# A hybrid encoder block on one core: DeltaNet scalings spread over half tiles, norm sums moved, w_out's raw buffers and the last norm's order

## The chip, the cores and the metric

The kernel runs on one core of a Trainium2 chip. The metric is the device time of one execution in microseconds (us); less is better. A core has the engines TensorE (PE, matmul; PEld is its weight load), VectorE (DVE), ScalarE (ACT), GpSimd (POOL) and SyncE (SP, which issues most transfers), each with an instruction stream of its own that it works off in order; semaphores tie the streams together. The transfers themselves are done by 16 DMA engines.

## The reference

One layer on 1024 positions of width 1024, in float32, and a last RMSNorm:

```python
h = rmsnorm(x, norm_mix_w)
qa, ka, va, za, ba, aa, qb, kb, vb, ga, gb = split(h @ w_in)
qa, ka, va = split(silu(causal_dwconv(cat(qa, ka, va), conv_qkv_w)))     # 4 heads of 128
qa, ka = l2norm(qa), l2norm(ka); beta = sigmoid(ba); g = -exp(a_log) * softplus(aa + dt_bias)
oa = rmsnorm(gated_delta_rule(qa, ka, va, g, beta), gdn_norm_w) * silu(za)
ob = chunk_band_attention(qb, kb, vb, rel_bias)                          # 8 heads of 64
x = x + (sigmoid(ga) * (oa @ w_branch_a) + sigmoid(gb) * (ob @ w_branch_b)) @ w_out
h = rmsnorm(x, norm_ffn_w); u = causal_dwconv(h @ w_up, conv_ffn_w) + conv_ffn_b
x = x + (silu(gate) * up) @ w_down                                       # gate, up = split(u)
return rmsnorm(x, norm_final_w)

def gated_delta_rule(q, k, v, g, beta):          # per head, chunks of 64 positions, n = 16
    G = cumsum(g); gam = exp(G)
    a_mat = beta * (k @ k.T) * exp(G_i - G_j) [i > j]
    w_c, uv_c = solve(a_mat + I, [beta * gam * k, beta * v])             # triangular
    p_c = (q @ k.T) * exp(G_i - G_j) [i >= j]; kd_c = k * exp(G_last - G)
    for each chunk:  u = uv_c - w_c @ s;  o = (q * gam) @ s + p_c @ u;  s = gam_last * s + kd_c.T @ u
```

## The kernel before, in words

Every large matmul is done as three with operands split in a high and a low part (`whi`, `wlo` of a weight, `BH`, `BL` of h). A weight tile of 128x1024 is loaded by SP (`wraw`), cast by ACT (`whi`, line 85) and subtracted by POOL (`wlo`, line 88, four instructions). Raw, high and low tiles come from one pool, `wst`, with two buffers for each of the tags `raw`, `hi` and `lo`; a load waits until the buffer that it takes has been read.

A *half tile* is 24 matmuls of 512 columns: one weight tile against half of the positions, into one `psph`. In the DeltaNet part the loop is `for h in range(-1, GH)`; in turn h the kernel emits the chain of head h, the preparation of head h+1 and, as filling between their steps, the projections and convolutions of head h+2, the output gate z of head h+1 and some branch gates. `n` counts the half tiles of a turn and `i_s = h + 1` picks from the tuples at the top of the file at which n a piece is emitted:

- `SCALE`, a dictionary by head: `gdn_scale(c, p)` (lines 555 to 561) multiplies one of eight pairs of chunks of the head's `Kd`, `Vs` and `nKs` by factors per row, four ACT instructions. A head in `SCALE` gets one p in each half tile from n on, placed behind the last `acc` or gate instruction on ACT. For a head not in it, `gdn_prep2` emits all eight behind the exponential `decT` (line 548).
- `QN`: when `gdn_qnorm` squares q (`sqq`, line 680) and sums it on PE (`psn`); `gdn_qnorm2` copies the sums (`sn`, 694) and sends them through DRAM (`dN`, `sx`, 696 and 699) to `sx`, which line 710 reads on DVE.
- `APP`, `OUT`, `LATE`: when the solved system is applied, the head's output is transposed (`oaT`) and the second decay factor is applied. Heads are counted from 0 in the code and from the first in the words here, so that the second and third head are 1 and 2.

The preparation of a head sends its matrix `nL` to DRAM (`dL`, four DMAs, line 534) and back in another layout (`Lr`, line 536). The triangular solve runs on DVE: 31 steps of `tmp` (583) and `Zt` (585), the first of which reads Lr. Between them DVE works off the chain of the head before: U (653), O (654) and S (658) for each chunk, which PE waits for in `pss` and `psws`, and the convolution: u (440), then ACT's `acc` (444), then three `acc` on DVE (446). A scheduler sets the order of each engine from priorities and dependences, so that a small move in the code moves many rows; near the end of the program the order is pinned as written.

`load_wout(k, pool)` (line 1073) loads and splits one of eight blocks of `w_out`, the last four behind the branch products (`psout` waits for their `woh`, `wol`). In the tail, the last four tiles of 128 positions get their second half's squares early and the first half's after its last matmuls; `final` (1797) makes the mean and takes the power -0.5 on POOL (`rsf`), and `finish` (1868) scales the two halves of the output (`ot`) on ACT and DVE and stores them.

Of the kernel before, what the change touches and what calls it, by code (L numbers as in the profile page):

```python
# [8 lines left out]
F32 = mybir.dt.float32  # L9
F32R = mybir.dt.float32r  # L10
BF16 = mybir.dt.bfloat16
AF = mybir.ActivationFunctionType
ALU = mybir.AluOpType
# [4 lines left out]
P = 128  # L18
D = 1024
KT = D // P  # L20
T = 1024
NT = T // P
HN = 512
# [5 lines left out]
EPS = 1e-6  # L29
# [6 lines left out]
OUT = (0, 3, 5, 3, 8)  # L36
APP = (12, 10, 10, 2)
TANH = (0,)
SCALE = {0: 2}
LATE = (9, 8, 8, 1)  # L40
APK = (4, 4, 3, None)
QN = (7, 5, 7, 5)
PR0 = 1
SOLVE0 = {3: 5, 4: 4, 5: 5, 6: 6, 7: 6, 8: 5}
GFILL = (6, 4, 5, 5, 4)
# [7 lines left out]
def hybrid_kernel(ctx: ExitStack, tc: tile.TileContext, a):  # L53
# [6 lines left out]
    def behind(key="mm"):  # L60

        return tc.issue_after(last[key])
# [3 lines left out]
    wst = ctx.enter_context(tc.tile_pool(name="wst", bufs=2))  # L66
    sml = ctx.enter_context(tc.tile_pool(name="sml", bufs=8))
# [339 lines left out]
    def zeros(t_):  # L407

        nc.sync.dma_start(t_, a["zeros"].partition_broadcast(P).rearrange("p (n t) -> p n t", t=P))
# [96 lines left out]
    def gdn_prep2(c):  # L506
# [41 lines left out]
        last["exp"] = nc.scalar.activation(decT.rearrange("p n j -> p (n j)"), psd2, AF.Exp).ins  # L548
        if h not in SCALE:
            with behind("exp"):  # L550
# [4 lines left out]
    def gdn_scale(c, p):  # L555
        h, Kd, nKs, Vs = c["h"], c["Kd"], c["nKs"], c["Vs"]
        for e in range(2):
            r = slice(e * CH, (e + 1) * CH)
            nc.scalar.activation(Kd[r, p, e, :], nKs[r, p, :], AF.Copy, scale=eg[r, 2, p, h:h + 1])
        nc.scalar.activation(nKs[:, p, :], nKs[:, p, :], AF.Copy, scale=c["nks"][:, p:p + 1])  # L560
        nc.scalar.activation(Vs[:, p, :], Vs[:, p, :], AF.Copy, scale=c["bv"][:, p:p + 1])
# [115 lines left out]
    def gdn_qnorm(c):  # L677

        sqq = gp.tile([P, NT, P], F32, tag="zs", name="sqq")
        nc.scalar.activation(sqq, c["WQ"][:, :, 64:192], AF.Square)  # L680
        psn = psc.tile([P, 256], F32, tag="c", name="psn")

        def sums():
            for j in range(4):
                mm(psn[j * 32:(j + 1) * 32], ones2[:, 0:32], sqq[:, 2 * j:2 * j + 2, :].rearrange("p n t -> p (n t)"),
                   start=True, stop=True)

        side.append(sums)
        c["psn"] = psn
# [32 lines left out]
    def gdn_out(c):  # L722
        h, O, zs = c["h"], c["O"], c["zs"]
        oaT = stg.tile([P, T], F32, tag="gt", name="oaT")
        for q in range(2):
            ps = psc.tile([P, HN], F32, tag="c", name="psoT")
            for i in range(4):
                nc.tensor.transpose(out=ps[:, i * P:(i + 1) * P], in_=O[:, 4 * q + i, :], identity=ident)
            s = slice(q * HN, (q + 1) * HN)
            pv = ps.rearrange("p (n e t) -> p n e t", e=2, t=CH)  # L730
            zv = zs[:, s].rearrange("p (n e t) -> p n e t", e=2, t=CH)
            ov = oaT[:, s].rearrange("p (n e t) -> p n e t", e=2, t=CH)
            for e in range(2):
                nc.vector.scalar_tensor_tensor(out=ov[:, :, e, :], in0=pv[:, :, 1 - e, :], scalar=gnw[:, 0:1],
                                               in1=zv[:, :, e, :], op0=ALU.mult, op1=ALU.mult)
        nc.sync.dma_start(dO[h], oaT)
# [26 lines left out]
    for h in range(-1, GH):  # L763
# [34 lines left out]
        while True:  # L798
            if h + 1 < GH and n == QN[i_s]:
                gdn_qnorm(cs[h + 1])  # L800
# [10 lines left out]
            if n == 0 and h < 0:  # L811
                for t_ in [*ptA, *zts, *(k_[:, :, j] for k_ in Kds for j in range(2))]:
                    zeros(t_)
            if h + 1 < GH and n == QN[i_s]:
                while side:
# [19 lines left out]
            if h >= 0 and n == OUT[i_s]:  # L835
                with tc.high_priority(offset=PRI), behind():
                    gdn_out(cs[h])
            if 0 <= n - SCALE.get(h + 1, n + 1) < NT:
                with behind("act"):
                    gdn_scale(cs[h + 1], n - SCALE[h + 1])  # L840
            n += 1
# [228 lines left out]
    wop = ExitStack()  # L1070
    wo1 = wop.enter_context(tc.tile_pool(name="wo1", bufs=1, reuse_waits="tile"))

    def load_wout(k, pool):
        raw = wst.tile([P, KT, P], F32, tag="raw", name="woraw")
        nc.sync.dma_start(raw.rearrange("p k c -> p (k c)"), a["w_out"][k * P:(k + 1) * P, :])
        hi = pool.tile([P, D], F32R, name=f"woh{k}")
        lo = pool.tile([P, D], F32R, name=f"wol{k}")
        split(raw.rearrange("p k c -> p (k c)"), hi, lo, nc.vector)
        return hi, lo
# [8 lines left out]
    wout = []  # L1088
# [32 lines left out]
    XT = [[xo.tile([P, 4, HN], F32R, name=f"XT{n}{x}") for x in "hl"] for n in (1, 2, 3)]  # L1121
    wo2 = wop.enter_context(tc.tile_pool(name="wo2", bufs=1, reuse_waits="tile"))
    for k in range(4, KT):
        wout.append(load_wout(k, wo2))
    psz.close()
    psx.close()
    psF = ctx.enter_context(tc.tile_pool(name="psF", bufs=8, space=PSUM, reuse_waits="tile"))
    h0, h1 = slice(0, HN), slice(HN, T)
# [4 lines left out]
    def ps_tile(name):  # L1133
        return psF.tile([P, HN], F32, tag="mm", name=name)
# [163 lines left out]
    V, S, G, Q = Pinned(nc.vector), Pinned(nc.scalar), Pinned(nc.gpsimd), Pinned(nc.sync)  # L1298
# [477 lines left out]
    fd = ctx.enter_context(tc.tile_pool(name="fd", bufs=1, reuse_waits="tile"))  # L1776
    W12.extend(fd.tile([P, HN], F32, name=f"W12_{f}") for f in range(3, FH))
    x2 = [fd.tile([P, D], F32, name=f"x2_{t}") for t in range(NT)]
# [11 lines left out]
    for b, s in (((0, 0), 6), ((1, 1), 16), ((0, 1), 27), ((1, 0), 45)):  # L1790
        for i in range(4):
            t, c = 4 * b[0] + i, slice(b[1] * HN, (b[1] + 1) * HN)
# [1 line left out]
    loads.append((50, wn, a["norm_final_w"].partition_broadcast(P)))  # L1794
    loads.sort(key=lambda x: x[0])

    def final(t, ssqs):

        ms = sml.tile([P, 1], F32, tag="ms", name="msf")
        V.tensor_scalar(out=ms, in0=ssqs[0], scalar1=1.0 / D, scalar2=EPS, op0=ALU.mult, op1=ALU.add)  # L1800
        for i, q_ in enumerate(ssqs[1:]):
            m2 = fd.tile([P, 1], F32, tag=f"ms{i}", name="msf", bufs=4)
            V.scalar_tensor_tensor(out=m2, in0=q_, scalar=1.0 / D, in1=ms, op0=ALU.mult, op1=ALU.add)
            ms = m2
        rs = sml.tile([P, 1], F32, tag="rs", name="rsf")
        G.tensor_tensor(out=rs, in0=ms, in1=mhalf[:, 0:1], op=ALU.pow)
        return rs

    s0s, ots = [], []
    jk = fd.tile([P, D], F32, name="jk")  # L1810

    def early_steps():

        for t in range(4, NT):
            s0 = fd.tile([P, 1], F32, tag="ssq0", name="ssqf", bufs=4)
            S.activation(jk[:, h1], x2[t][:, h1], AF.Square, accum_out=s0)
            s0s.append(s0)
            ot = fd.tile([P, D], F32, tag="ot2", name="ot", bufs=4)
            G.tensor_mul(ot[:, h1], x2[t][:, h1], wn[:, h1])
            ots.append(ot)  # L1820
            yield

    def norm_steps():

        ssq, rs = {}, {}
        for i in range(6):
            if i < 4:
                ssq[i] = sml.tile([P, 1], F32, tag="ssq", name="ssqf")
                S.activation(jk, x2[i], AF.Square, accum_out=ssq[i])
            if 1 <= i < 5:  # L1830
                rs[i - 1] = final(i - 1, [ssq[i - 1]])
            if i >= 2:
                t = i - 2
                ot = fd.tile([P, D], F32, tag="ot", name="ot", bufs=2)
                V.scalar_tensor_tensor(out=ot, in0=x2[t], scalar=rs[t], in1=wn, op0=ALU.mult, op1=ALU.mult)
                Q.dma_start(a["out"][t * P:(t + 1) * P, :], ot)
            yield
# [27 lines left out]
    t = NT - 1  # L1865
    V.tensor_tensor(out=x2[t][:, h0], in0=acc[0][3], in1=x2[t][:, h0], op=ALU.add)

    def finish(i, rs):
        t, ot = 4 + i, ots[i]
        S.activation(ot[:, h1], ot[:, h1], AF.Copy, scale=rs)  # L1870
        V.scalar_tensor_tensor(out=ot[:, h0], in0=x2[t][:, h0], scalar=rs, in1=wn[:, h0], op0=ALU.mult, op1=ALU.mult)
        for e in (h1, h0):
            Q.dma_start(a["out"][t * P:(t + 1) * P, e], ot[:, e])

    ssqs = [[s0] for s0 in s0s]
    rss = {}
    for i in range(4):
        t = 4 + i
        for ci, es in enumerate((h0,) if i < 3 else (slice(0, 256), slice(256, HN))):
            ps = ps_tile("psd") if i == 3 else acc[0][i]  # L1880
            for s in range(TAIL, NS):
                tc.keep_in_program_order(down_mm(ps[:, es], s, i, i == 3 and s == TAIL, s == NS - 1, es,
                                                 skip_group_check=i < 3))
            V.tensor_tensor(out=x2[t][:, es], in0=ps[:, es], in1=x2[t][:, es], op=ALU.add)
            s1 = fd.tile([P, 1], F32, tag=f"ssq1{ci}", name="ssqf", bufs=4)
            S.activation(jk[:, es], x2[t][:, es], AF.Square, accum_out=s1)
            ssqs[i].append(s1)
            if ci == 0:
                if i > 0:
                    rss[i - 1] = final(t - 1, ssqs[i - 1])  # L1890
                if i > 1:
                    finish(i - 2, rss[i - 2])
    rss[3] = final(NT - 1, ssqs[3])
    finish(2, rss[2])
    finish(3, rss[3])


def layout(inp):
# [60 lines left out]
```

## Time and profile before

| | |
|---|---|
| median of 3 runs | 1517.43 us (1517.19 to 1518.5) |
| the profiled execution | 1519.18 us; span of its instructions 1517.4 us |
| clock granted to TensorE, mean | 0.998 of full speed |
| busy: DVE, ACT, POOL | 1081.3, 724.8, 579.4 us |
| idle of PE before instructions that wait for DVE's U (L653) | 2.5 us in 5 places |

Rows of the time order read: start in us from the span's start, length in us, engine, line, operation, output<-inputs, shape, number, and in brackets the idle time before the instruction and what ended it. Rows that begin with "SPq" are transfers at their issue; rows with "DMA" have issue and time to landing. A row of the waits reads: who waits for whom, total us, times, longest. A group's row ends with busy us, mean ns of one, and idle before it.

### The profile page before, as it was taken

The page shows a single profiled execution, that of the slowest core. Times are in us where ns is not written, and L with a number is a line of the kernel's source. Part 1 is how long each engine was busy: PE and PEld are TensorE (multiplying, and loading weights), DVE is VectorE, ACT ScalarE, POOL GpSimd, SP SyncE. Part 2 cuts the span into 40 slices and gives each one's busy share as a digit, 9 for nine tenths or more (in the row PEclk, how much of TensorE's full clock was granted, in tenths as well). Part 3 has the DMA queues.
Part 4 walks back from the last instruction along what each step waited for, and adds up shares of the span by engine and source line. Part 5 has one row for each costly group of instructions (what it writes and reads, how often), then busy time and mean ns, then how long its engine had stood idle before and what let it go on. Part 6 is the DMA issues. An engine that isn't in the chain of part 4 may idle for free.

```text
span 1517.4 us, 21270 instructions
## 1 busy us (share of the span) xinstructions
PE 1500.7 (99%) x7667; PEld 1231.9 (81%) x7667; DVE 1081.3 (71%) x2161; ACT 724.8 (48%) x1412; POOL 579.4 (38%) x529
## 2 busy tenths in 40 slices
PE   9999999999999999999999999999999999999997
PEld 6878787777888888888878878888888888888886
DVE  6875857856547887966554577777777777887886
ACT  7645546373236665744223344444444444443344
POOL 1633324222110000002211278877777775223253
PEclk9999999999999999999999999999999999999999
DMA  9322221213131111215552222333333332875523
GB/s 344 104 74 67 70 77 46 78 48 117 43 107 45 37 46 37 65 63 169 174 160 104 84 88 86 104 104 105 104 104 105 104 104 81 284 261 167 179 89 141
DMA packets 84025, 165.74 MB, mean 109 GB/s; under 512 B 20160, under 2 KB 26064, under 8 KB 83920
## 3 DMA queue, kind: packets, MB, share of 16 engines
q1 hardware_dynamic: 83376, 163.34, 32.6%
q8 instruction: 60, 0.98, 0.3%
q10 hardware_dynamic: 544, 1.05, 0.2%
q14 instruction: 45, 0.37, 0.1%
HBM read 124.24 MB, written 40.12 MB: 108 GB/s over the span
## 4 chain that ended last, share of the span: by engine, by line
PE 74%; DVE 1%; ACT 1%; DMA 1%; issue 1%; POOL 0%; SPq 0%; POOLq 0%; ACTq 0%; DVEq 0%
PE psph L58 20%; PE psd L58 9%; PE pb L58 8%; PE pa L58 5%; PE psout L58 5%; PE pc L58 5%; PE psd L1641 5%; PE pb L1282 4%; PE pa L1282 3%; PE pc L1282 3%; PE pso L58 2%; PE pss L58 2%; PE psp L996 2%; PE pst L1170 0%; PE psws L58 0%
## 5 line engine op out<-in xcount | busy, mean ns | idle before, releaser
L88 POOL TENSOR_TENSOR wlo<-wraw,whi 128x256 fp32r<-128x256 f32 x132 | 107.3, 841 | 453.9 <-ACT whi L85 452.6
L58 PE MATMUL psph<-BH,whi 128*128 128x512 f32 x656 | 263.4, 402 | 0.7 <-DVE gt L188 0.4
L58 PE MATMUL psph<-BL,whi 128*128 128x512 f32 x656 | 262.2, 400 | 0.0
L58 PE MATMUL psph<-BH,wlo 128*128 128x512 f32 x656 | 260.7, 397 | 0.0
L1296 POOL TENSOR_TENSOR ol<-wraw,oh 128x512 fp32r<-128x512 f32 x110 | 150.5, 1386 | 6.6 <-ACT oh L1296 6.5
L58 PEld LDWEIGHTS psph<-BH,whi 128*128 128x128 f32 x656 | 123.6, 188 | 24.1 <-issue 2.8
L58 PEld LDWEIGHTS psph<-BH,wlo 128*128 128x128 f32 x656 | 123.7, 189 | 21.5
L58 PEld LDWEIGHTS psph<-BL,whi 128*128 128x128 f32 x656 | 123.8, 189 | 20.4
L1296 POOL TENSOR_TENSOR wraw<-wraw 128x512 f32<-128x512 f32 x86 | 119.0, 1384 | 4.9
L58 PE MATMUL psd<-wdl,ah 128*128 128x512 f32 (+1 forms) x311 | 120.4, 387 | 0.0
L1641 PE MATMUL psd<-wdh,al 128*128 128x512 f32 (+1 forms) x311 | 120.3, 387 | 0.0
L58 PE MATMUL psd<-wdh,ah 128*128 128x512 f32 (+1 forms) x311 | 119.4, 387 | 0.0
L1296 ACT CAST oh<-wraw 128x512 fp32r<-128x512 f32 x110 | 67.7, 619 | 103.7 <-POOL wraw L1296 103.6
L1296 POOL TENSOR_TENSOR al<-araw,ah 128x1024 fp32r<-128x1024 f32 (+1 forms) x26 | 65.6, 2522 | 134.7 <-ACT ah L1296 102.5
L1296 DVE TENSOR_TENSOR wdl<-W,wdh 128x512 fp32r<-128x512 f32 x77 | 86.9, 1166 | 23.6 <-ACT wdh L1296 23.5
L1296 ACT CAST ah<-araw 128x1024 fp32r<-128x1024 f32 (+1 forms) x39 | 40.6, 1040 | 104.4 <-PE psd L58 43.4
L1296 POOL TENSOR_TENSOR gl<-wraw,gh 128x512 fp32r<-128x512 f32 x42 | 56.2, 1340 | 68.7 <-ACT gh L1296 68.7
L1282 PE MATMUL pa<-BH,gh 128*128 128x512 f32 x176 | 68.6, 389 | 0.0
L58 PE MATMUL pa<-BH,gl 128*128 128x512 f32 x176 | 68.5, 389 | 0.0
L58 PE MATMUL pa<-BL,gh 128*128 128x512 f32 x176 | 68.5, 389 | 0.0
L58 PEld LDWEIGHTS psd<-wdh,ah 128*128 128x128 f32 x311 | 58.4, 188 | 12.0
L58 PEld LDWEIGHTS psd<-wdl,ah 128*128 128x128 f32 x311 | 58.4, 188 | 11.9
(349 smaller groups left out, 3818.0 us busy)
## 6 DMA issues: line engine op xcount, KB each, us to landing
wraw<-w_up SPq DMA_DIRECT2D x44, 512.0 KB, 5.5
wraw<-w_tiles SPq DMA_DIRECT2D x41, 512.0 KB, 3.7
araw<-dA SPq DMA_DIRECT2D x77, 256.0 KB, 3.0
dA<-yu SPq DMA_DIRECT2D x31, 512.0 KB, 2.8
W<-w_down SPq DMA_DIRECT2D x44, 256.0 KB, 4.3
xt<-x SPq DMA_DIRECT2D x16, 512.0 KB, 3.5
dG<-gt SPq DMA_DIRECT2D x16, 512.0 KB, 2.7
ta<-dG SPq DMA_DIRECT2D x16, 256.0 KB, 2.8
```

Source lines behind the costliest of these rows:

```text
L58: last["mm"] = nc.tensor.matmul(*args, **kw).ins
L88: nc.gpsimd.tensor_tensor(out=lo[:, k:k + 2], in0=src[:, k:k + 2], in1=hi.bitcast(F32)[:, k:k + 2], op=ALU.subtract)
L996: nc.tensor.transpose(out=psp[:, i * P:(i + 1) * P], in_=Sb[:, (i0 + i) * P:(i0 + i + 1) * P], identity=ident)
L1282: i = nc.tensor.matmul(ps, wh[:, k], xh[:, k], start=start and k == 0, stop=False, **kw)
L1296: return lambda *args, **kw: tc.keep_in_program_order(f(*args, **kw))
L1641: i = nc.tensor.matmul(ps, al[:, j, ts], wh[:, es], start=False, stop=stop, **kw)
```

## The change

Four things change:

- The scalings of the second and third head are emitted one p per half tile from n = 0 on (`SCALE = {0: 2, 1: 0, 2: 0}`); the fourth head's stay together.
- The third head's `gdn_qnorm` moves from n = 7 to n = 8 (`QN`).
- The raw tiles of w_out's blocks 6 and 7 (from 0) take buffers with the tags `hi` and `lo`.
- In the tail the square is scaled by 1/32 before it is summed, so that its sum is the mean; four small adds (`msp`) put EPS to the second half's means ahead of the last matmuls, and each tile has one add and one power. `finish` comes one tile earlier. The last tile's two quarters are squared and summed on DVE in one instruction, and the last store of a second half is issued by ACT (`S`) and no longer by SP (`Q`).

```diff
-SCALE = {0: 2}
+SCALE = {0: 2, 1: 0, 2: 0}
-QN = (7, 5, 7, 5)
+QN = (7, 5, 8, 5)
...
-    def load_wout(k, pool):
-        raw = wst.tile([P, KT, P], F32, tag="raw", name="woraw")
+    def load_wout(k, pool, tag="raw"):
+        raw = wst.tile([P, KT, P], F32, tag=tag, name="woraw")
...
-        wout.append(load_wout(k, wo2))
+        wout.append(load_wout(k, wo2, ("raw", "raw", "hi", "lo")[k - 4]))
...
-    def final(t, ssqs):
-        ms = sml.tile([P, 1], F32, tag="ms", name="msf")
-        V.tensor_scalar(out=ms, in0=ssqs[0], scalar1=1.0 / D, scalar2=EPS, op0=ALU.mult, op1=ALU.add)
-        for i, q_ in enumerate(ssqs[1:]):
-            m2 = fd.tile([P, 1], F32, tag=f"ms{i}", name="msf", bufs=4)
-            V.scalar_tensor_tensor(out=m2, in0=q_, scalar=1.0 / D, in1=ms, op0=ALU.mult, op1=ALU.add)
-            ms = m2
+    def root(ms):
         rs = sml.tile([P, 1], F32, tag="rs", name="rsf")
         G.tensor_tensor(out=rs, in0=ms, in1=mhalf[:, 0:1], op=ALU.pow)
         return rs
...
-        for e in (h1, h0):
-            Q.dma_start(a["out"][t * P:(t + 1) * P, e], ot[:, e])
-    ssqs = [[s0] for s0 in s0s]
-    rss = {}
+        (S if i == 3 else Q).dma_start(a["out"][t * P:(t + 1) * P, h1], ot[:, h1])
+        Q.dma_start(a["out"][t * P:(t + 1) * P, h0], ot[:, h0])
+    part = []
+    for i in range(4):
+        m_ = fd.tile([P, 1], F32, tag="ms0", name="msp", bufs=4)
+        V.tensor_scalar_add(m_, s0s[i], EPS)
+        part.append(m_)
+    rs = None
...
             V.tensor_tensor(out=x2[t][:, es], in0=ps[:, es], in1=x2[t][:, es], op=ALU.add)
-            s1 = fd.tile([P, 1], F32, tag=f"ssq1{ci}", name="ssqf", bufs=4)
-            S.activation(jk[:, es], x2[t][:, es], AF.Square, accum_out=s1)
-            ssqs[i].append(s1)
-            if ci == 0:
-                if i > 0:
-                    rss[i - 1] = final(t - 1, ssqs[i - 1])
-                if i > 1:
-                    finish(i - 2, rss[i - 2])
-    rss[3] = final(NT - 1, ssqs[3])
-    finish(2, rss[2])
-    finish(3, rss[3])
+            m2 = sml.tile([P, 1], F32, tag="ms", name="msf")
+            if i < 3:
+                s1 = fd.tile([P, 1], F32, tag="ssq10", name="ssqf", bufs=4)
+                S.activation(jk[:, es], x2[t][:, es], AF.Square, scale=D ** -0.5, accum_out=s1)
+                if i:
+                    finish(i - 1, rs)
+                V.tensor_tensor(out=m2, in0=s1, in1=ms, op=ALU.add)
+                rs = root(m2)
+            else:
+                V.tensor_tensor_reduce(out=jk[:, es], in0=x2[t][:, es], in1=x2[t][:, es], scale=1.0 / D, scalar=ms,
+                                       op0=ALU.mult, op1=ALU.add, accum_out=m2)
+            ms = m2
+    rs3 = root(ms)
+    finish(2, rs)
+    finish(3, rs3)
```

How the instructions move, at three places. The numbers behind the names count tiles and differ between the two kernels. First ACT in the second head's preparation; `decT` is the exponential, `zs` the first head's gate, `acc` the first step of a convolution. Before (the three scaling rows are repeated eight times in all):

```order
L548 ACTIVATE decT_1556<-psd2_1553 128x512
L559 ACTIVATE Kd1_368<-nKs_1397,eg_601 64x128 x2
L561 ACTIVATE Vs_1398<-Vs_1398,bv_1401 128x128
L560 ACTIVATE nKs_1397<-nKs_1397,nks_1403 128x128
...
L673 ACT_TABLE_LOAD
L673 ACTIVATE zs_1288<-zs_1288 128x512
L444 ACTIVATE acc_1846<-u_1842,prm_116 128x512
L85 CAST whi_1888<-wraw_1886 128x1024
```

and now:

```order
L548 ACTIVATE decT_1556<-psd2_1553 128x512
L85 CAST whi_1864<-wraw_1862 128x1024
L673 ACT_TABLE_LOAD
L673 ACTIVATE zs_1288<-zs_1288 128x512
L709 ACTIVATE jk_1749,sqo_1748<-O_1430 128x128 x2
L444 ACTIVATE acc_1814<-u_1810,prm_116 128x512
L709 ACTIVATE jk_1749,sqo_1748<-O_1430 128x128
L559 ACTIVATE Kd1_368<-nKs_1397,eg_601 64x128 x2
L561 ACTIVATE Vs_1398<-Vs_1398,bv_1401 128x128
L560 ACTIVATE nKs_1397<-nKs_1397,nks_1403 128x128
```

The cast of a weight goes from behind the scalings to a place ahead of them, and `acc` stands ahead of the first scaling.

SP at the same place; the `wraw` behind Lr takes the buffer of the weight that the cast above reads. Before:

```order
L192 DMA dG_87<-gt_1223 128x1024
L98 DMA wraw_1981<-w_tiles 128x1024
L534 DMA dL_1529<-nL_1526 32x8x32 x4
L536 DMA Lr_1534<-dL_1529 128x1x1024
L98 DMA wraw_2074<-w_tiles 128x1024
L98 DMA wraw_2139<-w_tiles 128x1024
```

and now:

```order
L192 DMA dG_87<-gt_1223 128x1024
L98 DMA wraw_1965<-w_tiles 128x1024
L534 DMA dL_1529<-nL_1526 32x8x32 x4
L98 DMA wraw_2066<-w_tiles 128x1024
L536 DMA Lr_1534<-dL_1529 128x1x1024
L98 DMA wraw_2139<-w_tiles 128x1024
```

A weight load has come between the stores dL and the load Lr; both places are the same in the third head's stage.

DVE in the tail, its last rows; `x2_6` and `x2_7` are the last two tiles, and `ISA` is the fused square and sum. Before:

```order
L1296 SCALAR_TENSOR_TENSOR ot_13460<-x2_5_12322,rsf_13789,wn_12347 128x512
L1296 TENSOR_TENSOR x2_7_12324<-psd_13818,x2_7_12324 128x256
L1296 TENSOR_SCALAR msf_13831<-ssqf_13501 128x1
L1296 SCALAR_TENSOR_TENSOR msf_13833<-ssqf_13806,msf_13831 128x1
L1296 SCALAR_TENSOR_TENSOR msf_13835<-ssqf_13829,msf_13833 128x1
L1296 SCALAR_TENSOR_TENSOR ot_13499<-x2_6_12323,rsf_13812,wn_12347 128x512
L1296 SCALAR_TENSOR_TENSOR ot_13503<-x2_7_12324,rsf_13837,wn_12347 128x512
```

and now:

```order
L1296 SCALAR_TENSOR_TENSOR ot_13460<-x2_5_12322,rsf_13785,wn_12347 128x512
L1296 TENSOR_TENSOR msf_13797<-ssqf_13798,msp_13747 128x1
L1296 TENSOR_TENSOR x2_7_12324<-psd_13807,x2_7_12324 128x256
L1296 ISA jk_12348,msf_13818<-x2_7_12324,msp_13749 128x256
L1296 ISA msf_13818 128x1
L1296 TENSOR_TENSOR x2_7_12324<-psd_13820,x2_7_12324 128x256
L1296 ISA jk_12348,msf_13831<-x2_7_12324,msf_13818 128x256
L1296 ISA msf_13831 128x1
L1296 SCALAR_TENSOR_TENSOR ot_13499<-x2_6_12323,rsf_13805,wn_12347 128x512
L1296 SCALAR_TENSOR_TENSOR ot_13503<-x2_7_12324,rsf_13833,wn_12347 128x512
```

The output's scaling for tile 5 has moved ahead of both quarters of tile 7, and the squares of these quarters are DVE's.

More of the change, by code (lines that the diff above doesn't have):

```diff
@@ L1807, in final @@
         return rs
+    def final(ssq):
+        ms = sml.tile([P, 1], F32, tag="ms", name="msf")
+        V.tensor_scalar(out=ms, in0=ssq, scalar1=1.0 / D, scalar2=EPS, op0=ALU.mult, op1=ALU.add)
+        return root(ms)
     s0s, ots = [], []
@@ L1815, in early_steps @@
             s0 = fd.tile([P, 1], F32, tag="ssq0", name="ssqf", bufs=4)
-            S.activation(jk[:, h1], x2[t][:, h1], AF.Square, accum_out=s0)
+            S.activation(jk[:, h1], x2[t][:, h1], AF.Square, scale=D ** -0.5, accum_out=s0)
             s0s.append(s0)
@@ L1830, in norm_steps @@
             if 1 <= i < 5:
-                rs[i - 1] = final(i - 1, [ssq[i - 1]])
+                rs[i - 1] = final(ssq[i - 1])
             if i >= 2:
@@ L1871, in finish @@
         V.scalar_tensor_tensor(out=ot[:, h0], in0=x2[t][:, h0], scalar=rs, in1=wn[:, h0], op0=ALU.mult, op1=ALU.mult)
-        for e in (h1, h0):
-            Q.dma_start(a["out"][t * P:(t + 1) * P, e], ot[:, e])
-    ssqs = [[s0] for s0 in s0s]
-    rss = {}
+        (S if i == 3 else Q).dma_start(a["out"][t * P:(t + 1) * P, h1], ot[:, h1])
[6 more added lines that the diff above has]
+    rs = None
     for i in range(4):
         t = 4 + i
-        for ci, es in enumerate((h0,) if i < 3 else (slice(0, 256), slice(256, HN))):
+        ms = part[i]
+        for es in (h0,) if i < 3 else (slice(0, 256), slice(256, HN)):
             ps = ps_tile("psd") if i == 3 else acc[0][i]
```

## The prediction

> **What bounds the kernel now.** I read the first part of the page, then the table of TensorE's waits, then the time order of the engines around each wait. The busy line comes first.
>
> ```profile
> PE 1500.7 (99%) x7667; PEld 1231.9 (81%) x7667; DVE 1081.3 (71%) x2161; ACT 724.8 (48%) x1412; POOL 579.4 (38%) x529
> PE pss L58 <- DVE U L653: 2.5, 5, 0.9
> PE psn L58 <- ACT sqq L680: 0.9, 1, 0.9
> PE psout L58 <- ACT woh L85: 0.7, 2, 0.5
> PE psph L58 <- DVE gt L188: 0.4, 1, 0.4
> ```
>
> PE is busy for all but 16.7 us of the 1517.4 us span, and the change takes no matmul away. It can gain only in PE's waits and behind PE's last matmul. The four wait rows (total us, times, longest) are the ones the edits touch; together they are 4.5 us idle.
>
> **The scalings of the second and third head.** The second head's stage is at 145 to 200 us, the third's at 236 to 300 us; the order of work is the same in both. PE first, where the wait shows:
>
> ```profile
> 162.05 0.39 PE L58 MATMUL psph<-BL,whi 128*128 128x512 f32 x1
> 162.28 0.39 PE L58 MATMUL psph<-BH,wlo 128*128 128x512 f32 x1
> 163.06 0.49 PE L58 MATMUL pss<-U,Kd 128*128 128x128 f32 x2 [0.40 <-DVE U L653]
> 165.76 0.39 PE L58 MATMUL psph<-BH,wlo 128*128 128x512 f32 x1
> 166.52 0.49 PE L58 MATMUL pss<-U,Kd 128*128 128x128 f32 x2 [0.37 <-DVE U L653]
> ...
> 253.17 0.49 PE L58 MATMUL pss<-U,Kd 128*128 128x128 f32 x2 [0.41 <-DVE U L653]
> ```
>
> A 512-column matmul frees PE for the next one 0.23 us after it starts (162.05 to 162.28). The two `pss` start 0.78 and 0.76 us after the matmul ahead, so the two stalls cost 0.55 + 0.53 = 1.1 us; that is some 0.15 more for each than the idle time in brackets (0.55 against 0.40), and I add this restart to other waits below. What made U late:
>
> ```profile
> 147.05 0.80 ACT L559 ACTIVATE Kd<-nKs,eg 64x128 f32<-64x128 f32 x2
> 158.73 0.39 ACT L560 ACTIVATE nKs<-nKs,nks 128x128 f32<-128x128 f32 x1
> 161.25 0.71 ACT L444 ACTIVATE acc<-u,prm 128x512 f32<-128x512 f32 x1
> 155.91 0.67 DVE L440 TENSOR_TENSOR u<-psph,rb 128x512 f32<-128x512 f32 x1
> 162.06 0.75 DVE L446 SCALAR_TENSOR_TENSOR acc<-u,prm,acc 128x512 f32<-128x512 f32 x1 [0.78 <-ACT acc L444]
> 162.74 0.27 DVE L653 TENSOR_TENSOR U<-psws,U 64x128 f32<-64x128 f32 x1
> ```
>
> The first and last of the 32 scalings stand at 147.05 and 158.73 (two of the 32 to the first row, one to the last). Behind them, ACT reaches `acc` L444 only at 161.25, although its input u was there at 155.91 + 0.67 = 156.6. DVE then stands 0.78 us before its first `acc` L446, and U, queued behind it, reaches PE late. After the change ACT has no scaling there: it comes to `acc` at 156.6 and has done it by 157.3, and the three L446 are spread over early steps of the solve. The `acc` wait of 0.78 is gone; what is late next is DVE's own work, since it still has the same three 0.75 us L446 to fit between U's, so some stalls remain. I keep 0.4 of the 1.1 (about half of one stall for each of two places where an L446 stands ahead of U, 2 x 0.2) and take 0.7 per stage, **1.4** for both. The upper bound is all of it, 2.2. The lower bound comes from what is moved on SP's queue. The third head's stage has the same wait (253.17, 0.41) and the same ends. The next rows are read as one chain.
>
> ```profile
> 148.64 1.06 POOL L478 TENSOR_TENSOR gsl<-cn,glo 128x512 fp32r<-128x512 f32 x1
> 202.18 2.83 POOL L88 TENSOR_TENSOR wlo<-wraw,whi 128x256 fp32r<-128x256 f32 x4 [6.67 <-ACT whi L85]
> 151.88 0.56 SPq L536 DMA_DIRECT2D Lr<-dL  x1
> 156.97 0.15 DVE L583 TENSOR_TENSOR tmp<-Zt,Lr 128x8 f32<-128x8 f32 x1
> DMA to landing us min/median/max: 3.4/3.4/3.4
> 206.79 0.38 SPq L98 DMA_DIRECT2D wraw<-w_tiles  x1
> 325.31 5.52 DMA Lr<-dL
> 330.86 0.18 DVE L583 TENSOR_TENSOR tmp<-Zt,Lr 128x8 f32<-128x8 f32 x1 [0.98 <-DMA Lr<-dL]
> ```
>
> Before, Lr is issued at 151.88 and lands 3.4 us later (the landing row is Lr's, of 150 to 157 us), at 155.3; the first solve step reads it at 156.97, so 1.7 us are spare. After, a weight load stands ahead of Lr. It waits until POOL has split the weight whose buffer it takes: POOL is free of gsl at 149.7, the four wlo take 2.83, so 152.5. With 0.38 for the issue, Lr is issued at about 152.95, 1.1 later than before. Alone it would land at 156.35, 0.6 early. With 512 KB just ahead of it I add 0.7, between nothing and the 2.1 by which the slowest Lr of the trace (5.52, the row at 325.31) is longer than 3.4: 157.05, within 0.1 of its use. So I cost it at nothing, by the 0.6 that cover it; without cover the row at 330.86 is the price, 0.98 on DVE, and if it all reaches PE a stage loses 0.98 instead of gaining 0.7. Half of it reaching PE and only half a stall won (0.25 - 0.5) is my lower bound, -0.25 per stage, -0.5 for both.
>
> The scalings themselves are not fewer: 8 x 4 for each head, one p (0.80 + 0.40 + 0.39, some 1.4 us with the overlap) in each half tile of 24 matmuls x 0.23 = 5.5 us, on an engine that is 48% busy. Their readers come with the apply at half tile 10; the last scaling is at 7, so two half tiles, 11 us, cover them.
>
> **The norm sums of the third head.** PE waited 0.9 us for sqq, once; the cause is ACT's:
>
> ```profile
> 284.64 1.06 ACT L680 ACTIVATE sqq<-WQ 128x1024 f32<-128x1024 f32 x1 [0.78 <-DVE oaT L734]
> ```
>
> One half tile later, the buffer has long been released when sqq starts. The wait row's 0.9 and the restart make **1.1** (0.93 + 0.16). The bounds are 0 to 1.1. What follows on this path, the copy sn and the DMAs dN and sx, is 5.5 us later and goes past the solve's dZ and zt on SP; sx L710 is moved on DVE behind both ptA, some 4 us, and a weight load now stands ahead of the DMAs sx, so that DVE may stand about 1 us there. The next product that PE needs from it is 2 us further on. I cost this at nothing by those 2 us.
>
> **The gate wait.** The second head's `psph` waits 0.4 for `gt` L188, since DVE stood before it:
>
> ```profile
> 194.73 0.17 DVE L710 TENSOR_SCALAR sx<-sx 128x8 f32<-128x8 f32 x1 [1.05 <-DMA sx<-dN]
> ```
>
> After the change L710 comes two solve steps later (about 1.7 us, each step two rows of 0.4 and a gap), though a scaling ahead of sn on ACT delays the data by 1.4. I take **0.4** of 0.4 + 0.15; bounds 0 and 0.55.
>
> **The weights of w_out.** The raw tiles of its seventh and eighth block take buffers of the split weights instead of waiting for raw ones:
>
> ```profile
> 787.43 4.60 DMA woraw<-w_out
> 791.00 0.50 PE L58 MATMUL psout<-woh,BH 128*128 128x512 f32 x1 [0.53 <-ACT woh L85]
> 793.15 0.50 PE L58 MATMUL psout<-woh,BH 128*128 128x512 f32 x1 [0.15 <-ACT woh L85]
> ```
>
> The load at 787.43 lands at 792.03, just ahead of PE's wait at 793.15. The freed buffers let both be issued near 781, 5 us sooner, so that wait goes: 0.15 + 0.15. The wait at 791.00 is DVE's and ACT's order of splits as much as the data, and the code order of splits stays; I take only 0.1 of its 0.68. Sum **0.4**; the upper bound is 0.53 + 0.15 + 2 x 0.15 + 0.2 for a further short stall of lo = 1.2. Below, the loads could crowd the ta and tb loads of the last products; I allow the largest single wait of this row again, -0.5.
>
> **The tail.** Behind PE's last matmul:
>
> ```profile
> 1509.36 0.28 PE L1641 MATMUL psd<-wdh,al 128*128 128x256 f32 x1
> 1509.79 0.75 DVE L1296 SCALAR_TENSOR_TENSOR ot<-x,rsf,wn 128x512 f32<-128x512 f32 x1
> 1510.45 0.42 DVE L1296 TENSOR_TENSOR x<-psd,x 128x256 f32<-128x256 f32 x1
> 1511.68 0.99 POOL L1296 TENSOR_TENSOR rsf<-msf,mhalf 128x1 f32<-128x1 f32 x1 [0.74 <-DVE msf L1296]
> 1512.71 0.75 DVE L1296 SCALAR_TENSOR_TENSOR ot<-x,rsf,wn 128x512 f32<-128x512 f32 x1 [0.44 <-POOL rsf L1296]
> 1513.45 0.84 SPq L1296 DMA_DIRECT2D out_dram<-ot  x2
> L979 DVE CUSTOM_DVE_ANT_0 Sb<-pss,bias 128x256 f32<-128x256 f32 x8 | 3.3, 408 | 0.0
> ```
>
> The last quarter's x waits until 1510.45 only because DVE is in ot of the tile two before. That ot goes ahead, so x starts at about 1509.9. The fused square and sum on DVE is not in the trace; the nearest is a custom instruction over the same 128x256, 0.41, and at worst it is this and a read of the sum of ACT's length, 0.6. From 1509.9: x 0.42 (overlapped to 0.35), square 0.41, sum read 0.1, so the root starts at 1510.8 instead of 1511.68, 0.9 earlier. The root (0.99), ot (0.75) stay. The two last stores leave one after another now, 0.42 each; on two queues the last leaves 0.4 sooner, which makes 1.3. The landing of the stores may not follow in full, so I take **1.2**. Bounds: 1.4, all and a little of the earlier stores; 0, if the store on ACT's queue lands late, by these rows (size, median us from issue to landing; the last is the output's stores):
>
> ```profile
> dA<-yu SPq DMA_DIRECT2D x31, 512.0 KB, 2.8
> dA<-yu ACTq DMA_DIRECT2D x2, 512.0 KB, 4.4
> out_dram<-ot SPq DMA_DIRECT2D x8, 256.0 KB, 2.4
> ```
>
> The same transfer took 1.6 us longer from ACT's queue, but only twice and among other traffic; the tail's own stores, half the size, land in 2.4, and I go by them. The smaller edits here (four one-column adds ahead, one add less per tile) lie beside matmuls that DVE waits for.
>
> By the rows of ACT's queue the tail is worth nothing and the sum would be 3.3, 1514.1. The Trainium skill, "DMA: Bandwidth & Descriptors", section "Issuing engines are not separate DMA queues", says against them that transfers of all issuing engines share the same DMA engines and that another issuer saves only the sequencer's time; by it the store's part is the 0.42 of one issue, neither more nor less, and the sum 4.5.
>
> **The sum.** 1.4 + 1.1 + 0.4 + 0.4 + 1.2 = 4.5 us. The profiled execution took 1519.18 (span 1517.4), which gives 1514.7; the median of the three runs, 1517.43, is 1.75 below it, so the forecast is 1517.43 - 4.5 = **1512.9**. Ends of the terms: -0.5 + 0 + 0 - 0.5 + 0 = -1.0 and 2.2 + 1.1 + 0.55 + 1.2 + 1.4 = 6.45, so 1518.4 to 1511.0 if all fell together. About 0.2%, 3.0 us, is what a measurement here can tell from no change.
>
> **Rivals.**
>
> B. Lr lands late in both stages. If it takes 5.52 instead of 4.1 from 152.95, it lands at 158.5, 1.5 behind the solve's first step; each stage then loses about 0.5 instead of winning 0.7, 2 x 1.2 = 2.4. The total gain is 2.1: 1515.3, not told from no change. For it speaks the row at 325.31, against it that this is the longest of the trace.
>
> The Trainium skill, the same page, section "Two DMAs through the same engine are not ordered", says that within one queue of one DMA engine descriptors start in order, though pipelined. By that Lr's data start only behind the weight's 512 KB, and B is what happens if they drain as slowly as there; no row before shows the pair, a weight load with Lr right behind it.
>
> C. The other side: the weight load holds SP. It waits for wlo on POOL, and that for whi on ACT. If ACT reached whi only behind `acc`, as it does before (161.25 + 0.71, then about 1.06 for 128x1024 as at 284.64, then wlo 2.83 and the issue 0.38), Lr would be issued at 166.2 and land at 169.6, 12.7 behind its step. The solve's 31 steps must be over before the head's next matmuls, so nearly all of that reaches PE: 2 x 12 = 24 us, less 3.1 of the other edits, 21 slower, 1538. Up to an issue of Lr at 153.6 nothing is lost (156.97 - 3.4); from 155.1 the loss of 1.55 in each stage outweighs the 3.1, and from 156.6 it is slower by over 3.0. Against it: behind decT, ACT's next instruction in the new order is whi.
>
> D. The stalls of the two stages are DVE's own work and stay: 4.5 - 1.4 = 3.1, and with a tail of half the size 2.5: 1514.9, also not told from no change.
>
> **How the numbers follow.** The forecast holds 0.69, B 0.16, D 0.09, C 0.06. B and D count as same, with a part of the forecast's own spread below 3.0 us balanced by D's above it. The range reaches from 1511.2, near the best sum, over B and D to 1516.2, where the lower bounds of two terms (a stage that loses, a store that lands late) meet.
>
> **What would show it.** Right: of the five `pss` waits for U, the four of the second and third head's stages gone or shorter, ACT's `acc` L444 right behind u; the `psn` wait gone; DVE's first solve step without a wait for Lr; the last root 1.2 us behind the end of PE's last matmul, both last stores issued together. Wrong: a wait of DVE for Lr near 157 us and in the third head's stage likewise (B), SP's Lr issued behind 155 (C), L653 waits unchanged with ACT on time (D), or new PE waits in the half tiles that now hold scalings, where a late Silu delays a product.

## The result and the profile after

The changed kernel takes 1514.19 us (median of 13 runs, 1513.11 to 1515.29) against 1518.09 us of the kernel before on the same chips (median of 13). One run of the kernel before took 1650.4 us; the ratio leaves it out, and the median of the other 12 is 1517.76. The ratio is 0.9976, 95% interval [0.9969, 0.9982]: 3.6 us faster, where 4.5 were forecast. The profiled execution took 1514.96 us, 4.2 less than the one of before; 0.4 of the 4.2 stand ahead of everything that was changed (a matmul at 144.31 us is at 143.90 now), so the profile shows about 3.8.

Some rows of TensorE's waits in the changed kernel (total us, times, longest):

```profile
PE pss L58 <- DVE U L653: 2.5, 3, 0.8
PE psph L58 <- ACT wf L85: 0.7, 1, 0.7
PE psws L58 <- DVE S L658: 0.6, 2, 0.4
PE psout L58 <- DVE wol L91: 0.3, 1, 0.3
PE psph L58 <- DVE gt L188: 0.3, 1, 0.3
```

The row of `psn` is gone, and `psout` has 0.3 for 0.7. But `pss` still waits 2.5 us for U, in three places and no longer in five: in the stages of the second and of the third head one wait of 0.8 has taken the place of two of 0.4, and in the fourth head's one of 0.8 that of one of 0.9. The second head's stage, rows of SP, ACT, DVE and PE:

```profile
152.09 0.35 SPq L98 DMA_DIRECT2D wraw<-w_tiles  x1
152.61 0.56 SPq L536 DMA_DIRECT2D Lr<-dL  x1
DMA to landing us min/median/max: 5.2/5.2/5.2
156.22 0.72 ACT L444 ACTIVATE acc<-u,prm 128x512 f32<-128x512 f32 x1 [3.03 <-DVE u L440]
157.86 0.17 DVE L583 TENSOR_TENSOR tmp<-Zt,Lr 128x8 f32<-128x8 f32 x1 [1.22 <-DMA Lr<-dL]
158.16 0.27 DVE L653 TENSOR_TENSOR U<-psws,U 64x128 f32<-64x128 f32 x1
158.94 0.75 DVE L446 SCALAR_TENSOR_TENSOR acc<-u,prm,acc 128x512 f32<-128x512 f32 x1
157.29 0.40 PE L58 MATMUL psph<-BL,whi 128*128 128x512 f32 x1
158.49 0.49 PE L58 MATMUL pss<-U,Kd 128*128 128x128 f32 x2 [0.80 <-DVE U L653]
```

ACT does `acc` right behind u, as forecast, and DVE no longer waits for it (the row at 158.94 has no bracket). In its place DVE stands 1.22 us for Lr, which landed 5.2 us after its issue (the landing row is Lr's), and U (158.16) stands behind that first solve step. PE then starts `pss` 1.20 us after the matmul ahead, a stall of 0.97 where before there were 0.55 + 0.53. TensorE's shift, the time by which the same matmul comes earlier than in the kernel before, grows from 0.40 to 0.71 over this stage. So the stage won 0.3 in all, short restarts counted in. The third head's stage reads the same (Lr issued at 241.75 and landed at 246.97, stall 0.98, shift from 1.38 to 1.69).

DVE's L710, ahead of the gate near 200 us, has no wait for its data any more, and the stall of PE behind it is gone:

```profile
195.37 0.15 DVE L710 TENSOR_SCALAR sx<-sx 128x8 f32<-128x8 f32 x1
```

A stall that the kernel before did not have stands just ahead of the moved norm sums (`psn`, now at 289.02):

```profile
284.40 0.74 DVE L446 SCALAR_TENSOR_TENSOR acc<-u,prm,acc 128x512 f32<-128x512 f32 x1
287.32 0.68 DVE L188 TENSOR_TENSOR gt<-psph,rb 128x512 f32<-128x512 f32 x1
287.50 0.39 PE L58 MATMUL psph<-BH,wlo 128*128 128x512 f32 x1
288.15 0.47 PE L58 MATMUL psph<-BH,whi 128*128 128x512 f32 x1 [0.26 <-DVE gt L188]
```

PE starts 0.65 after the matmul ahead, 0.42 lost: DVE was in one half tile's oaT and three `acc` and came late to `gt`.

At w_out PE no longer waits for `woh`, but a wait for `wol` has come:

```profile
786.79 0.50 PE L58 MATMUL psout<-wol,BH 128*128 128x512 f32 x1 [0.31 <-DVE wol L91]
```

The tail, rows of PE, DVE and POOL and then a store:

```profile
1505.98 0.28 PE L1641 MATMUL psd<-wdh,al 128*128 128x256 f32 x1
1506.62 0.42 DVE L1296 TENSOR_TENSOR x<-psd,x 128x256 f32<-128x256 f32 x1
1507.08 0.48 DVE L1296 CUSTOM_DVE_ANT_0 jk<-x,msf 128x256 f32<-128x256 f32 x1
1507.65 0.99 POOL L1296 TENSOR_TENSOR rsf<-msf,mhalf 128x1 f32<-128x1 f32 x1 [1.18 <-DVE msf L1296]
1508.68 0.75 DVE L1296 SCALAR_TENSOR_TENSOR ot<-x,rsf,wn 128x512 f32<-128x512 f32 x1 [0.44 <-POOL rsf L1296]
1509.43 0.40 ACTq L1296 DMA_DIRECT2D out_dram<-ot  x1
```

From the end of the last matmul (1506.26) to the end of the span (1513.2) there are 6.9 us; before there were 7.8 (1509.64 to 1517.4). The root starts 1.39 us behind PE's end, 2.04 before. The root is not all that changed here. The eight stores of the last four tiles were all issued behind PE's end before, and the DMA engines then worked without a gap from 1510.5 to 1516.1. Now two of them are issued ahead of PE's end, and the engines have a gap of 0.3 us just before the last pair. Busy tenths of the DMA engines, before (1509 to 1518 us in 40 slices) and now (1500 to 1514 us in 40 slices):

```profile
DMA  0000002999999999999999999999999100000000
DMA  0000000000000049994069999999259993000000
```

How much of the 0.8 is the earlier root's and how much the earlier stores', no experiment separates.

### The profile page after: what moved, and what is told of

The parts are those of the page before. It is cut to its first block, busy times and chain, and to the rows that moved or that the text cites. A ratio compares the mean times of both kernels' runs of the same rounds, so it can differ in the third digit from the quotient of the medians.

```text
span 1513.2 us, 21266 instructions
## 1 busy us (share of the span) xinstructions
PE 1498.5 (99%) x7667; PEld 1232.3 (81%) x7667; DVE 1079.3 (71%) x2163; ACT 723.7 (48%) x1408; POOL 575.7 (38%) x529
## 4 chain that ended last, share of the span: by engine, by line
PE 74%; ACT 2%; DVE 1%; issue 1%; DMA 0%; POOL 0%; SPq 0%; POOLq 0%; ACTq 0%; DVEq 0%
PE psph L58 20%; PE psd L58 9%; PE pb L58 8%; PE psout L58 5%; PE pa L58 5%; PE pc L58 5%; PE psd L1641 5%; PE pb L1282 4%; PE pa L1282 3%; PE pc L1282 3%; PE pso L58 2%; PE pss L58 2%; PE psp L996 2%; PE pst L1170 0%; PE psws L58 0%
## 5 line engine op out<-in xcount | busy, mean ns | idle before, releaser
L1641 PEld LDWEIGHTS psd<-wdh,al 128*128 128x128 f32 x311 | 58.4, 188 | 11.9
```

The source lines that it names most:

```text
L1641: i = nc.tensor.matmul(ps, al[:, j, ts], wh[:, es], start=False, stop=stop, **kw)
```

## The experiments

All were timed against the kernel before on the same chip. The changed kernel's ratio is 0.9976 [0.9969, 0.9982].

**Lr ahead of the weight load.**

```diff
-        nc.sync.dma_start(raw, src)
+        late = loads_from[0] is not None and loads_from[0] >= 3
+        with behind("lr") if late else nullcontext():
+            nc.sync.dma_start(raw, src)
+        if loads_from[0] is not None:
+            loads_from[0] += 1
...
-        nc.sync.dma_start(Lr, ...)
+        last["lr"] = nc.sync.dma_start(Lr, ...).ins
+        loads_from[0] = 0 if h in (1, 2) else None
```

Weight loads are counted from the load Lr of the second and third head on; from the fourth on, a load is issued behind Lr (`behind`).

> The changed kernel with one move: the weight load that stands between the dL stores and the load Lr in the second and third head's stages is issued behind Lr. Theory (the weight load ahead makes Lr late, 5.2 us to landing, and DVE's first solve step waits 1.2 us for it): Lr is issued near 151.4 and lands before its first use at 156.3, DVE does not wait for it, the single pss stall of 0.97 us in each of the two stages falls to 0.2 or less, and the kernel is 1.2 to 1.8 us faster than the changed one, 5 us faster than before (ratio 0.9967). Rival (the stall is DVE's own work and would only be met elsewhere): Lr lands early, the DVE wait for it goes, but pss or psws stalls of 0.8 us or more a stage remain and the kernel is within 0.4 us of the changed one (ratio 0.9975). Second rival (the two transfers share the bandwidth whichever is first): Lr still takes 4.5 us or more and DVE waits 0.3 us or more.

Measured: 1512.64 us, ratio 0.9968 [0.9956, 0.9981], and 2.3 us less span than the changed kernel's profile. SP, DVE and PE at the same place:

```profile
151.54 0.56 SPq L541 DMA_DIRECT2D Lr<-dL  x1
152.20 0.53 SPq L101 DMA_DIRECT2D wraw<-w_tiles  x1
Lr<-dL SPq DMA_DIRECT2D x1, 512.0 KB, 3.8
wraw<-w_tiles SPq DMA_DIRECT2D x1, 512.0 KB, 4.5
156.63 0.15 DVE L589 TENSOR_TENSOR tmp<-Zt,Lr 128x8 f32<-128x8 f32 x1
157.35 0.40 PE L58 MATMUL psph<-BL,whi 128*128 128x512 f32 x1
157.59 0.39 PE L58 MATMUL pss<-U,Kd 128*128 128x128 f32 x2
```

Lr takes 3.8 us with the weight right behind it and 5.2 with the weight ahead; it lands at 155.3, 1.3 before its step. Of the 2.5 us by which it lands earlier, 1.1 are the earlier issue and 1.4 the shorter time to landing. DVE does not wait, `pss` starts 0.24 behind the matmul ahead of it, and all that is left in each stage is one psws stall of 0.15. By TensorE's shift each of the two stages now wins 1.4 over the kernel before (0.34 to 1.74 and 2.40 to 3.80). The theory is shown; both rivals fall, the one that the stall was DVE's own work and the one that the order of two equal transfers would not matter.

**The scalings in a burst again.**

```diff
-SCALE = {0: 2, 1: 0, 2: 0}
+SCALE = {0: 2}
```

> The changed kernel with the scalings of the second and third head in one burst again (SCALE = {0: 2}); all else as changed. Theory (spreading the scalings took out two DVE waits for acc, but the late Lr gave nearly all of it back): the two pss stalls of 0.55 and 0.53 us per stage are back in place of one of 0.97, Lr lands in 3.4 us, and the kernel is slower than the changed one by 0.2 to 0.5 us (ratio to before 0.9978). The gate stall of 0.5 us near 200 us, which the changed kernel does not have, comes back too if it belongs to the scalings (then 0.9 us slower in all, ratio 0.9982). Rival (spreading won what was forecast, 1.4 us): slower by 1.4 us, ratio 0.9985.

Measured: 1515.54 us, 0.9986 [0.9977, 0.9995]. The two `pss` stalls per stage are back (0.56 and 0.53; 0.57 and 0.54), and so is the gate stall of 0.50 at 199 us:

```profile
PE pss L58 <- DVE U L653: 2.5, 5, 0.9
PE psph L58 <- DVE gt L188: 0.7, 2, 0.4
198.81 0.39 PE L58 MATMUL psph<-BH,wlo 128*128 128x512 f32 x1
199.53 0.47 PE L58 MATMUL psph<-BH,whi 128*128 128x512 f32 x1 [0.34 <-DVE gt L188]
```

The gate stall at 199 us belongs to the scalings. The second place of the `gt` row is PE's stall near 288.9 us, ahead of the moved sums, which stays. The spans differ by only 0.7 us (1513.9 and 1513.2), but this profile was 0.7 ahead of the changed kernel's at 150 us already, where their work is the same; at that place the profiles of all runs differ by up to 1.2. From there to 320 us TensorE's shift gives 1.4 for the spread scalings: 0.6 in the two stages, 0.6 at the gate, the rest at `psn` and `gt`. The medians' ratios give 1.5, with intervals that overlap. So the size is the rival's; the make-up is the theory's, with more at both places than I had expected.

**The norm sums at half tile 7 again.**

```diff
-QN = (7, 5, 8, 5)
+QN = (7, 5, 7, 5)
```

> The changed kernel with the third head's norm sums at half tile 7 again. Theory (the psn wait of 1.1 us went, but the DVE work that it had covered came out as a gate stall of 0.42 us one half tile on): the psn stall of about 1.1 us is back, the gate stall at 287.5 is gone, and the kernel is 0.7 us slower than the changed one (ratio to before 0.9981). Rival (the new gate stall belongs to the scalings, not to the moved sums): both stalls are there, 1.1 us slower than changed (ratio 0.9983).

Measured: 1517.33 us, ratio 1.0 [0.9991, 1.0009]; the whole gain is gone, 3.6 us where I had expected 0.7. Its profile:

```profile
283.33 1.06 ACT L680 ACTIVATE sqq<-WQ 128x1024 f32<-128x1024 f32 x1 [1.05 <-DVE oaT L734]
281.91 0.39 PE L58 MATMUL psph<-BH,wlo 128*128 128x512 f32 x1
284.44 0.42 PE L58 MATMUL psn<-sqq,ones 128*32 128x256 f32 x4 [2.15 <-ACT sqq L680]
```

The stall is 2.3 us, twice that of before: PE arrives 2.5 us earlier than before (281.9 against 284.4), 2.0 of them since the stalls ahead are gone, but sqq, which waits for oaT, starts only 1.3 us earlier (283.33 against 284.64). Most of what is won ahead is lost here. The stall at `gt` near 288 is gone, so it belongs to the moved sums. The span is 1.2 us longer than the changed kernel's; the median is 3 us longer, and the runs spread over 1515.81 to 1519.41. Where the rest goes no profile shows.

**The scalings alone.** The kernel before with `SCALE = {0: 2, 1: 0, 2: 0}` and nothing else.

> The kernel before with the scalings of the second and third head spread, and nothing else of the change. Theory (the spread scalings pull TensorE ahead of the chain that leads to sqq, so that without the later norm sums the psn wait eats what they win): Lr lands 1 us late in both stages, one pss stall of 0.6 to 1.0 in each in place of two of 0.55, no gate stall near 200 us, a psn stall of 2.0 to 2.4 us in place of 1.1, in all 0.3 us faster to 0.6 us slower than before (ratio 0.9998 to 1.0004). Rival (the parts add up without touching each other): 0.9 us faster, ratio 0.9994 or less, and a psn stall of 1.1 us as before.

Measured: 1518.6 us, ratio 1.0004 [0.9995, 1.0013], again with a wide spread (1516.66 to 1519.97; the profiled execution took 1517.73).

```profile
PE pss L58 <- DVE U L653: 2.3, 3, 0.9
PE psn L58 <- ACT sqq L680: 2.1, 1, 2.1
```

The `psn` stall is 2.29 us here too, the gate stall near 200 us is gone, and DVE stands 1.06 and 1.17 us for Lr in the two stages. This is as expected. Alone the spread scalings gain nothing; the parts of the change do not add up one by one.

**w_out's raw buffers as before.**

```diff
-        wout.append(load_wout(k, wo2, ("raw", "raw", "hi", "lo")[k - 4]))
+        wout.append(load_wout(k, wo2, "raw"))
```

> The changed kernel with all four last raw tiles of w_out in raw buffers again. Theory (the earlier loads are worth what the shift of TensorE between 784 and 795 us shows, 0.9 us): stalls of 0.29, 0.69 and 0.33 us at psout are back in place of 0.29 and 0.47, the kernel is 0.6 to 0.9 us slower than the changed one (ratio to before 0.9981). Rival (only the last small stall belongs to the loads, as forecast, 0.4 us): ratio 0.9978.

Measured: 1514.64 us, 0.998 [0.9971, 0.9988], which the times don't tell from the changed kernel. In the profile the `psout` stalls are 0.30, 0.51 and 0.18, 0.99 together, against 0.29 + 0.47 = 0.76 in the changed one, and TensorE falls back against it by 0.58 over the block. So the buffers are worth 0.2 to 0.6, nearer to the rival. The last two loads are issued at 783.72 and 784.85, and the first cast behind them waits 3.9 us for its data; in the changed kernel they are issued at 778.37 and 778.79, and no cast waits. The 0.9 which before and after differ by at this place is not the tags' alone: the experiment with the scalings alone, which has the old buffers, wins 0.4 there.

**The old tail.** Norm, squares and stores of the end as in the kernel before; the rest as changed.

> The changed kernel with the tail of before. Theory (the new tail is worth 0.8 us: from the end of TensorE's last matmul to the end of the span there were 7.8 us before and 7.0 after): 7.8 us again, the kernel 0.8 us slower than the changed one (ratio to before 0.9981). Rival (the tail is worth the 1.2 us of the forecast and the profile of before was taken by chance with a short tail): 8.2 us behind the last matmul, ratio 0.9984.

Measured: 1515.2 us, 0.9985 [0.9976, 0.9994]. PE's last matmul ends at 1506.38, the span at 1514.1: 7.7 us, as before. The new tail is worth 0.8 by the profiles and 1.4 by the medians' ratios, with intervals that overlap.

**The last store on SP.**

```diff
-        (S if i == 3 else Q).dma_start(a["out"][t * P:(t + 1) * P, h1], ot[:, h1])
+        Q.dma_start(a["out"][t * P:(t + 1) * P, h1], ot[:, h1])
```

> The changed kernel with the last store of a second half issued by SP again and no longer by ACT; the rest of the new tail stays. Theory (another issuing queue saves one issue, 0.4 us, but the last two stores share the same engines and drain together, so that less reaches the end): the last store leaves 0.4 us later and the span behind the last matmul is 0.1 to 0.4 us longer than the 7.0 us of the changed kernel. Rival (a store on ACT's queue lands later, as the two transfers dA did, 4.4 against 2.8 us): the span behind the last matmul gets shorter by 0.5 us or more with both on SP.

Measured: 1514.4 us, 0.998 [0.9971, 0.9989], not told from the changed kernel. The two stores leave one after another,

```profile
1509.16 0.81 SPq L1296 DMA_DIRECT2D out_dram<-ot  x2
```

the last at 1509.59, yet from PE's end (1505.99) to the end of the span (1512.8) there are 6.8 us, no more than the 6.9 with ACT's queue. The issue that was saved did not reach the end. In both runs the DMA engines move the two stores, 512 KB together, in 1.5 us without a gap (1510.3 to 1511.8 with ACT's queue, 1510.0 to 1511.5 here), so the second store's data do not wait for its later issue. That is neither the theory's gain nor the rival's 0.5.

**The fourth head's dL on two queues**, on top of the first experiment.

```diff
-            nc.sync.dma_start(dL[b].rearrange("n r c -> r n c"), ...)
+            (nc.scalar if b % 2 and h == 3 else nc.sync).dma_start(dL[b].rearrange("n r c -> r n c"), ...)
```

> The kernel with Lr ahead of the weight load (the first experiment), and for the fourth head two of its four dL stores issued by ACT and no longer by SP, so that Lr can be issued some 0.9 us earlier there. Theory (in every stage Lr's landing against the first solve step is what decides): DVE's wait of 0.9 us for Lr near 328 us and the pss stall of 1.0 us behind it go, 0.7 to 1.0 us faster than the first experiment (ratio to before 0.9962). Rival (this stage is bound by DVE's solve and chain, a stall taken out comes back in the next psws): the pss stall goes, but other stalls in the stage grow by as much, same time as the first experiment (0.9968).

Measured: 1512.43 us, 0.9967 [0.9955, 0.998], as the first experiment.

```profile
PE pss L58 <- DVE U L659: 0.6, 3, 0.2
PE psB L58 <- DMA zt<-dZ: 0.4, 1, 0.4
323.89 0.17 DVE L589 TENSOR_TENSOR tmp<-Zt,Lr 128x8 f32<-128x8 f32 x1 [0.18 <-DMA Lr<-dL]
```

DVE's wait for Lr falls from 0.88 to 0.18 and the `pss` stall of 1.0 goes. But the stalls of that stage together only fall from 2.6 to 1.8 us (0.6, 0.35, 0.3 and 0.3 stand later in it), and `psB` now waits 0.4 for the solved blocks. By TensorE's shift 0.4 are won up to 356 us, and less than 0.1 is left of them at 640. The rival holds here: in the fourth head's stage the chain and the solve on DVE are the limit.

**The last piece over 128 columns**, on top of the first experiment: the last tile's first half is cut at 384 and no longer at 256.

> The kernel with Lr ahead of the weight load (the first experiment), and the last tile's first half cut after 384 columns and no longer after 256, so that the work behind the last matmul is over 128 columns. Theory (x, square and sum of the last piece are in a row behind TensorE's end): they shrink from 0.42 and 0.48 us to about 0.25 and 0.3, the span behind the last matmul is 0.3 us shorter. Rival (DVE is still busy with the first piece when TensorE ends, since 384 columns of x and square take 1.1 us while the last matmuls of 128 columns take less): no gain or a loss of up to 0.3 us.

Measured: 1512.37 us, 0.9967 [0.9954, 0.9979]. From PE's end (1504.03) to the end of the span (1510.5) there are 6.5 us, 0.45 less than in the first experiment (1503.98 to 1510.9). The effect is there in the profile, too small for the times.

**Together**: Lr first, the narrow last piece and both stores on SP; and then OUT[2] = 4 on top.

> The first experiment (Lr ahead of the weight load) with the cut of the last tile after 384 columns and both last stores on SP. Theory (the two tail edits add up: 6.92 us behind the last matmul in the first experiment, less 0.45 for the narrow last piece and 0.1 for the store): 6.3 to 6.5 us behind the last matmul, ratio to before 0.9965. Rival (with both stores on SP the earlier last piece is lost in the second issue): 6.8 us or more, 0.9968.

> The kernel of the experiment before, with the second head's output (four oaT products on DVE) emitted one half tile earlier in the third head's stage (OUT[2] 5 to 4). Theory (the gate stall of 0.4 us near 286 us is DVE standing behind oaT and three acc of one half tile): the oaT products stand ahead of them, the stall is 0.1 us or gone, 0.3 us faster (ratio 0.9963). Rival (O is not ready that early, or DVE is full there too): a psoT or psph stall of 0.4 us or more appears one half tile earlier, same time or slower.

Measured: 1512.72 us, 0.9967 [0.9955, 0.998], and with OUT[2] = 4 1511.77 us, 0.9962 [0.995, 0.9975]. Behind PE's end both take 6.4 us, as expected; the first of the two is not told from the first experiment by its time. With OUT[2] = 4 the gate stall of 0.37 near 286 us is gone and none has come a half tile earlier. The last is the fastest median of all, 5.8 us below the kernel before, though its interval reaches over that of the first experiment.

## Why the prediction was right, and where it was not

The time was inside the range and the sign right; the sum of 4.5 came out as 3.6. By the shift of TensorE between the two profiles, step by step:

| step | forecast | profile |
|---|---|---|
| two stages, `pss` and `psws` | 1.4 | 0.6 |
| `psn`, less the new gate stall | 1.1 | 0.5 |
| gate stall near 200 us | 0.4 | 0.65 |
| w_out | 0.4 | 0.9 (0.2 to 0.6 by the undoing) |
| tail | 1.2 | 0.8 |

The shifts are read at matmuls that stand at 144.31, 175.03, 234.99, 269.90, 300.05, 783.06 and 797.06 us before and at 143.90, 174.33, 233.62, 268.22, 297.90, 780.66 and 793.74 now. Another 0.3 came at places where I had changed nothing. That the total is within 0.9 of the sum is partly luck: the stages, `psn` and the tail brought 1.8 less, the gate, w_out and the other places 1.0 more.

- **The step that failed** is the cover of Lr, in the largest term. I had Lr issued at 152.95 and landing at 157.05, with 0.7 added for the weight load ahead; it was issued at 152.61 and took 5.2 us, to 157.84, so 1.8 were added. The 0.6 of cover did not do, and DVE stood 1.22 us. This is rival B's mechanism, with 0.16 of the chances, and it is shown by moving the load: 3.8 us to landing and no stall. Its price I had wrong the other way: the stage did not lose 0.5, it won 0.3, since the two waits for `acc` did go and only one wait for Lr came. Had the cover held, each stage would have won about 1.4, as in the first experiment, more than the upper bound of 1.1 and not 0.7: the remaining stalls that I laid to DVE's own work (rival D too) were not there.
- The Trainium skill, "DMA: Bandwidth & Descriptors", section "Two DMAs through the same engine are not ordered", has descriptors of one queue start in order on an engine. The two orders agree with that: Lr takes 3.8 us ahead and 5.2 behind, and the weight pays in turn, 3.6 us ahead and 4.5 behind. I quoted the rule and still let the nearest single row decide.
- Rival C did not come: whi came right behind decT, and the weight load was issued at 152.09, 0.4 earlier than I had it.
- `psn`: the wait went, but I named only what hid the later sums, not what DVE would be late for next. That was `gt`, 0.42, gone when oaT comes a half tile earlier. And I took the two edits as independent; with the scalings spread and the sums left at 7 the stall is 2.3, so the moved sums protect the scalings' gain as well as their own. By the term alone the edit would have been undersized.
- Gate: right in cause, and shown by the second experiment; 0.5 to 0.65 for 0.4, since nothing is left of it.
- w_out: right in size by the undoing. PE's waits for `woh` went with the loads, which are issued 8 us sooner, where I had 5; a stall of 0.47 stayed at this place, now for `wol` on DVE.
- Tail: the root came 1.39 us behind PE's end, where I had 1.2 (square and sum 0.48 + 0.08, x at 1506.62 behind the first quarter's sum and not behind PE). The 0.4 for the second issuing queue did not come: with both stores on SP the end is no later. Here the Trainium skill, the same page, section "Issuing engines are not separate DMA queues", allows the sequencer's time as the most to be saved. The runs show none of it at the end of the span.

## What to carry to other kernels

When a change moves instructions on a queue, price the wait of each transfer that is now behind another of its size (here 512 KB landed 1.4 us later behind 512 KB than ahead of them), and compare it with the slack at its first reader; if it does not fit, swap the two in the order. When several stalls stand in a row on one busy engine's chain, taking out the first pulls the others tighter: undo each part from the whole, and not only add each to the old kernel, before saying what it is worth. Work out what the engine that was waiting will be late for next, since that is where part of the gain comes to light again.

## What the runs showed of the hardware that I had not expected

Two 512 KB transfers issued 0.5 to 0.7 us apart on one queue, in the second and third head's stages of all profiles that have such a pair: the one ahead takes 3.5 to 3.9 us to landing, the one behind 4.3 to 5.4. But a lone Lr also took 5.4 in the fourth head's stage (issued at 323.17, landed at 328.62) and 3.8 there when two of the four stores ahead of it went over ACT's queue; why is open. The eight stores of 256 KB at the end of the kernel before kept the DMA engines busy without a gap for 5.6 us. The fused square and sum takes 0.48 us over 128x256 and 0.35 over 128x128, with a read of the sum of 0.08.
